# A chunked recurrence's triangular inverses: blocks of 16 in place of 32, a further merge, and the transfers on GpSimd's queue

## The chip, the cores and the metric

One core of one Trainium2 chip runs the whole layer in float32. The metric is the device time of one execution in microseconds. Three runs of the kernel before gave 1290.92, 1291.6 and 1295.13; the median is 1291.6.

## The reference

```python
def reference(x, ...):                        # x: (1, 1024, 1024), one layer
    h = rmsnorm(x, norm_mix_g); p = h @ w_in
    p_rwkv = p[..., :1792] + (token_shift(p_rwkv) - p_rwkv) * shift_mu
    y_rwkv = rwkv7_group(p_rwkv, ...)         # 8 heads of 64
    y_conv = conformer_conv_group(p[..., 1792:], ...)   # GLU, 31 taps, 512 channels, LayerNorm, SiLU
    x = x + concatenate([y_rwkv, y_conv]) @ w_out
    h = rmsnorm(x, norm_mlp_g)
    x = x + square(relu(h @ w_ff1)) @ w_ff2   # 1024 -> 4096 -> 1024
    return rmsnorm(x, norm_final_g)

def rwkv7_recurrence(r, decay, k, v, a, b):   # one step of 1024, per head
    sa = einsum('bhvk,bhk->bhv', S, a_t)
    S = S * w_t + sa ⊗ b_t + v_t ⊗ k_t
    y = einsum('bhvk,bhk->bhv', S, r_t)
```

The recurrence is what the change is about.

## The kernel before

The recurrence is done in chunks of 64 tokens, 16 chunks in a row. Inside a chunk the rank-one updates are collected in a unit triangular matrix of 64 by 64 for each head, whose inverse Th is needed before the chunk can be applied to the state. The eight heads are two groups, g = 0 and 1, of four heads (two head pairs p each); the tokens are two halves, h = 0 and 1, of eight chunks.

The stages, and what leaves each:

- `in_proj` multiplies the normalised input by a block of 128 columns of w_in, with three products of high and low halves (names hh, hl of the input, wh, wl of the weights), into a PSUM bank (ca, cb, ya, yb, ...). `mix_block` makes r, k and v of a pair from it, `conv_block(0..3)` the gated channels h2 of the convolution. Each projection's h goes into 48 long DVE operations per block, the taps (`do_taps`), which sum into `acc`.
- `decays` and `stage1(p, h)`, four pairs by two halves: from r, k, v the triangular products (AM, of KB and AR) and other factors. They go to DRAM: am_d (triangular blocks), lk_d, v_d, bon_d, n2_d (norms). These stores stand on `nc.sync`, SP's queue.
- `solve(g, (0, 1))`, once for each group when the pairs of that group are done: the tile Q holds 128 blocks of 32 by 32, one block on a partition (two halves by two diagonal blocks by 8 chunks by 4 heads). Thirty steps of two DVE operations each (L528 a product into Qt, L530 a sum) invert them; L524 and L532 scale by the norms. Q comes from am_d, nup from n2_d, the result goes to qd_d.
- `merge(g, h)`: reads two 32-blocks (QS) and the block off the diagonal (MX), transposes the first (QT), and joins them with 32 + 32 matmuls of 32 by 32 (MX·QT, copied to PT, then PT·QS) into a 64 by 64 inverse in th_d. Transfers of solve and merge alternate between `nc.sync` and `nc.scalar`.
- `step(g)`: one chunk of one group's chain: `fetch` (LK, rhs, and TA, which holds Th) on `nc.sync`, then matmuls L1·rhs, a copy to SR, Th·R (the rows SR,TA: the hop with th), a copy to rhs, KB·rhs, and a DVE addition that gives the next rhs; results y to y_d. A chain is 16 steps in a row.
- `conv_norm` transposes all four blocks' `acc` (rows ident,acc), then the output projection (w_out in 128-row pieces), the MLP, and the last norm follow.

What sets the order: a scheduler places all instructions at build time by priorities (`tc.high_priority`, where solve and merges of both groups have offset HP, chain steps HP and 2·HP) and by data; each engine then runs its list in that order, and each DMA queue its own. The calls are written so: conv_block(2), solve(0), merge(0, 0), merge(0, 1), steps of chain 0 between the projections of pairs 2 and 3, conv_block(3), solve(1), merge(1, 0), and steps and taps up to merge(1, 1) and conv_norm. Taps written behind a solve are tied behind it (`gate["solve"]`, set by the solve's last operation). The pool `mp` gives r, k, v, AM, kt, kd and the like their buffers: AM has two, kt (shared with vt) one.

Of the kernel before, what the change touches and what calls it, by code (L numbers as in the profile page):

```python
# [18 lines left out]
P = 128  # L19
# [16 lines left out]
EB = 1  # L36
# [16 lines left out]
def hymba_layer(ctx: ExitStack, tc: tile.TileContext, a: dict, out: bass.AP):  # L53
# [361 lines left out]
    factors = {}  # L415

# [23 lines left out]
    def stage1(p, h):  # L440
# [15 lines left out]
        nc.sync.dma_start(out=n2_d[p // 2, h, :, 2 * (p % 2):2 * (p % 2) + 2, :].rearrange("c r s -> r c s"), in_=n2.rearrange("r (c s) -> r c s", c=8))  # L456
# [7 lines left out]
        for i in range(2):  # L464
            hs = slice(64 * i, 64 * i + 64)
            AM = mp.tile([P, 8, P], F32, name="AM", bufs=2)
            for q in range(2):
                b1 = bank("s1")
                for c in range(4):
                    b1.mm(b1.t[:, c * P:(c + 1) * P], KB[hs, 4 * q + c].rearrange("p j t -> p (j t)"), AR[hs, 4 * q + c, :], True, True)  # L470
                V.tensor_tensor(AM[:, 4 * q:4 * q + 4, :], b1.t.rearrange("p (c t) -> p c t", c=4),
                                mask[:, None, :].to_broadcast([P, 4, P]), op=ALU.mult)
            nc.sync.dma_start(out=am_d[:, p // 2, cs, 2 * (p % 2) + i, :], in_=AM[0:64])
            nc.sync.dma_start(out=lk_d[64:128, p // 2, cs, 2 * (p % 2) + i, :], in_=AM[64:128])
        for i in range(2):
            nc.sync.dma_start(out=lk_d[0:64, p // 2, cs, 2 * (p % 2) + i, :], in_=AR[64 * i:64 * i + 64])
        for q in range(2):
            kd = mp.tile([P, 4, P], F32, name="kd", bufs=1)
# [7 lines left out]
            nc.sync.dma_start(out=lk_d[:, p // 2, 8 * h + 4 * q:8 * h + 4 * q + 4, 4 + p % 2, :], in_=kt)  # L486
# [5 lines left out]
        for e in range(2):  # L492
            nc.sync.dma_start(out=v_d[:, p // 2, cs][:, e::2, p % 2, :], in_=vt[64 * e:64 * e + 64])
# [5 lines left out]
        nc.sync.dma_start(out=bon_d[:, 4 * h:4 * h + 4, p, :], in_=v.rearrange("p (q t) -> p q t", q=4))  # L499
# [9 lines left out]
    def solve_blocks(g, hs):  # L509

        R = 64 * len(hs)
        Q = sv.tile([P, 32, 32], F32, name="Q", bufs=1)[0:R]
        nup = small.tile([P, 32], F32, name="nup", bufs=1)[0:R]
        for k, h in enumerate(hs):
            for bl in range(2):
                p0, sl = k * 64 + bl * 32, slice(bl * 32, bl * 32 + 32)
                (nc.sync, nc.scalar)[bl].dma_start(
                    out=Q[p0:p0 + 32], in_=am_d[sl, g, 8 * h:8 * h + 8, :, sl].rearrange("s c n t -> (c n) s t"))
                nc.scalar.dma_start(out=nup[p0:p0 + 32], in_=n2_d[g, h, :, :, sl].rearrange("c n s -> (c n) s"))
        tmp = sv.tile([P, 256], F32, name="Qt", bufs=1)[0:R]  # L520
# [3 lines left out]
        V.tensor_tensor(Q, Q, nup[:, None, :].to_broadcast([R, 32, 32]), op=ALU.mult)  # L524
        for s in range(1, 31):
            n = 31 - s
            o = tmp[:, 0:s * n].rearrange("p (s t) -> p s t", s=s)
            V.tensor_tensor(o, Q[:, 0:s, s:s + 1].to_broadcast([R, s, n]),  # L528
                            Q[:, s:s + 1, s + 1:32].to_broadcast([R, s, n]), op=ALU.mult)
# [207 lines left out]
    def step(g):  # L737
# [4 lines left out]
        with tc.high_priority(offset=(1 + g) * HP):  # L742
# [8 lines left out]
            if c % 2 == 1:  # L751
# [608 lines left out]
```

## Time and profile before

| what | value |
|---|---|
| median of three runs | 1291.6 us |
| the profiled execution | 1291.95 us, span 1290.2 us |
| mean granted TensorE clock | 0.961 |
| instructions | 20800 |
| DMA on SP's, ACT's (hardware) queues | 181192 and 13056 packets |
| DMA on GpSimd's (software) queue | 128 packets |
| HBM traffic | 110.23 MB read, 49.84 MB written |

PE is TensorE's matmuls, PEld its weight loads, DVE VectorE, ACT ScalarE, POOL GpSimd, SP the engine that only issues transfers. A row of a timeline has start, duration, engine, line, operation, out<-in and shape; in a window row stand the busy time of each engine and the count in that stretch, then the clock that the throttle granted, the share of DMA and GB/s. The chain that ended last gives start, duration and what it was. Most of the work on PE is in single rows L96, the helper for matmuls (L99 that for transposes), so the tile names tell them apart.

### The profile page before, as it was taken

The page shows a single profiled execution, that of the slowest core. Times are in us where ns is not written, and L with a number is a line of the kernel's source. Part 1 is how long each engine was busy: PE and PEld are TensorE (multiplying, and loading weights), DVE is VectorE, ACT ScalarE, POOL GpSimd, SP SyncE. Part 2 cuts the span into 40 slices and gives each one's busy share as a digit, 9 for nine tenths or more (in the row PEclk, how much of TensorE's full clock was granted, in tenths as well). Part 3 has the DMA queues.
Part 4 walks back from the last instruction along what each step waited for, and adds up shares of the span by engine and source line. Part 5 has one row for each costly group of instructions (what it writes and reads, how often), then busy time and mean ns, then how long its engine had stood idle before and what let it go on. Part 6 is the DMA issues. An engine that isn't in the chain of part 4 may idle for free.

```text
span 1290.2 us, 20800 instructions
## 1 busy us (share of the span) xinstructions
PE 1217.5 (94%) x8107; PEld 1052.2 (82%) x8107; DVE 944.8 (73%) x1639; ACT 558.0 (43%) x1001; POOL 107.4 (8%) x57
## 2 busy tenths in 40 slices
PE   5999999998999688999999899999997999999996
PEld 4999898887888577999988788888876788888885
DVE  6479696789549945664668766665459898897997
ACT  6432433333441166333468455455562333333344
POOL 1000000000000000000000000000015234242310
PEclk9999999997997586999999999999999999999999
DMA  5213426455464555734225454443276425232003
GB/s 191 58 50 98 125 62 176 113 139 123 118 168 130 129 143 165 216 111 123 78 88 184 152 164 153 150 146 109 87 268 217 142 66 164 65 101 79 17 1 131
DMA packets 194475, 161.44 MB, mean 125 GB/s; under 512 B 54386, under 2 KB 153784, under 8 KB 194376
## 3 DMA queue, kind: packets, MB, share of 16 engines
q1 hardware_dynamic: 181192, 157.90, 41.5%
q10 hardware_dynamic: 13056, 2.13, 0.9%
q8 instruction: 64, 1.05, 0.3%
q14 instruction: 35, 0.29, 0.1%
q0 software_dynamic: 128, 0.08, 0.0%
HBM read 110.23 MB, written 49.84 MB: 124 GB/s over the span
## 4 chain that ended last, share of the span: by engine, by line
PE 61%; DVE 9%; DMA 4%; ACT 2%; issue 1%; SPq 0%; ACTq 0%; DVEq 0%
PE ps L96 27%; PE yb L96 9%; PE ya L96 8%; PE cb L96 7%; PE ca L96 6%; PE pr L96 3%; DVE bl L852 2%; DVE al L852 2%; DVE sA L1190 1%; DVE x L1221 1%; PE ps L99 1%; DMA woraw<-in_w_out_dram 1%; DMA th_d<-QS 1%; DVE Q L530 1%; DVE Qt L528 1%
## 5 line engine op out<-in xcount | busy, mean ns | idle before, releaser
L851 ACT ACTIVATE ah<-sA 128x1024 fp32r<-128x1024 f32 x32 | 33.9, 1061 | 120.9 <-PE yb L96 48.0
L96 PE MATMUL cb<-hh,wh 128*128 128x256 f32 x248 | 72.8, 293 | 1.5 <-ACT hh L243 1.5
L96 PE MATMUL cb<-hl,wh 128*128 128x256 f32 x248 | 73.0, 294 | 0.3 <-DVE hl L244 0.3
L96 PE MATMUL cb<-hh,wl 128*128 128x256 f32 x248 | 71.8, 290 | 0.0
L96 PE MATMUL ps<-bh,ah 128*128 128x512 f32 x168 | 64.5, 395 | 5.6 <-ACT ah L851 3.5
L96 PE MATMUL ps<-bh,al 128*128 128x512 f32 x168 | 65.0, 391 | 3.2 <-DVE al L852 3.2
L96 PE MATMUL ps<-bl,ah 128*128 128x512 f32 x168 | 66.3, 395 | 1.5 <-DVE bl L852 1.5
L96 PE MATMUL yb<-hh,wh 128*128 128x256 f32 x232 | 67.7, 292 | 0.0
L96 PE MATMUL yb<-hh,wl 128*128 128x256 f32 x232 | 66.6, 287 | 0.0
L96 PE MATMUL yb<-hl,wh 128*128 128x256 f32 x232 | 66.5, 287 | 0.0
L851 ACT ACTIVATE w1h<-s 128x512 fp32r<-128x512 f32 x64 | 40.3, 632 | 52.6 <-PE ps L96 34.0
L852 DVE TENSOR_TENSOR al<-sA,ah 128x1024 fp32r<-128x1024 f32 x32 | 48.0, 1506 | 19.6 <-ACT ah L851 19.5
L852 DVE TENSOR_TENSOR w1l<-s,w1h 128x512 fp32r<-128x512 f32 x64 | 44.0, 688 | 24.8 <-ACT w1h L851 24.7
L1190 POOL TENSOR_TENSOR sB<-B,B11e 128x1024 f32<-128x1024 f32 x4 | 12.5, 3134 | 541.6 <-DVE al L852 539.3
L96 PEld LDWEIGHTS cb<-hh,wh 128*128 128x128 f32 x248 | 48.5, 195 | 5.4 <-ACT hh L243 1.9
L871 ACT ACTIVATE c<-c 128x512 f32<-128x512 f32 x60 | 37.9, 632 | 33.4 <-DVE c L957 20.1
L96 PEld LDWEIGHTS cb<-hl,wh 128*128 128x128 f32 x248 | 48.3, 195 | 4.8 <-issue 4.0
L96 PEld LDWEIGHTS cb<-hh,wl 128*128 128x128 f32 x248 | 48.2, 194 | 2.3 <-issue 2.1
L851 ACT ACTIVATE w1h<-w1r 128x512 fp32r<-128x512 f32 x48 | 30.2, 631 | 42.5 <-PE ps L96 26.6
L852 DVE TENSOR_TENSOR w1l<-w1r,w1h 128x512 fp32r<-128x512 f32 x48 | 32.9, 688 | 19.7 <-ACT w1h L851 19.7
L96 PEld LDWEIGHTS yb<-hh,wh 128*128 128x128 f32 x232 | 44.6, 192 | 3.1 <-issue 2.1
L96 PEld LDWEIGHTS yb<-hh,wl 128*128 128x128 f32 x232 | 44.6, 192 | 1.6 <-issue 1.5
(472 smaller groups left out, 4029.4 us busy)
## 6 DMA issues: line engine op xcount, KB each, us to landing
w1r<-in_w_ff_dram SPq DMA_DIRECT2D x44, 512.0 KB
hid_d<-c SPq DMA_DIRECT2D x64, 256.0 KB
LK<-lk_d SPq DMA_DIRECT2D x32, 384.0 KB
A<-hid_d SPq DMA_DIRECT2D x24, 512.0 KB
B<-in_w_ff_dram SPq DMA_DIRECT2D x24, 512.0 KB
wraw<-in_w_in_dram SPq DMA_DIRECT2D x22, 512.0 KB
xt<-in_x_dram SPq DMA_DIRECT2D x8, 512.0 KB
lk_d<-AR SPq DMA_DIRECT2D x16, 256.0 KB
```

Of the source, the lines that this page charges most:

```text
L96: return self._order(PE.matmul(o, lhsT=lhsT, rhs=rhs, start=start, stop=stop, skip_group_check=more))
L99: self._order(PE.transpose(o, in_, identity))
L528: V.tensor_tensor(o, Q[:, 0:s, s:s + 1].to_broadcast([R, s, n]), Q[:, s:s + 1, s + 1:32].to_broadcast([R, s, n]), op=ALU.mult)
L530: V.tensor_tensor(Q[:, 0:s, s + 1:32], Q[:, 0:s, s + 1:32], o, op=ALU.add)
L851: S.activation(hi, src, AF.Copy)
L852: V.tensor_tensor(lo, src, hi.bitcast(F32), op=ALU.subtract)
L871: S.activation(c, c if src is None else src, AF.Relu)
L1190: engine.tensor_tensor(t, x, y, op=op)
L1221: V.tensor_tensor(o, o, banks[t].t, op=ALU.add)
```

## The change

It does three things.

The solve takes blocks of 16. A partition's 32 by 32 block now holds two diagonal blocks of 16, and one DVE operation handles both (views Q16, four dimensions). There are 14 steps in place of 30. The upper half off the diagonal stays zero: Qf is cleared once by GpSimd and only the diagonal blocks are loaded, with eight transfers in place of four.

The merge has a first stage. AD holds three blocks from am_d (the two 32-blocks and the one off the diagonal, twelve loads in place of four). 64 matmuls 32 by 32 (AD·QT), a copy, 64 matmuls 32 by 16 (AD·QS) and a masked addition (`upper` keeps the rows of the first 16) make 32-blocks of the 16s; a second transpose and the 32 + 32 matmuls of before follow. So 192 matmuls for 64 in each of four merges.

All stores of stage 1, all transfers of solve and merges, and the stores of y to y_d are issued by `G.dma_start`, GpSimd's queue: twelve for each of eight stage-1 blocks, 16 for each solve, 17 for each merge, twelve of y. `fetch`, with the loads of Th into TA, stays on SP. kd shares a buffer with Ei.

The diff, cut to its core:

```diff
+    Qf = sv.tile([P, 1056], F32, name="Q")
+    G.memset(Qf, 0.0)
+    Q32 = Qf[:, 0:1024].rearrange("p (s t) -> p s t", t=32)
+    Q16 = Qf.rearrange("p (b r) -> p b r", b=2)[:, :, 0:512].rearrange("p b (s t) -> p b s t", t=32)[:, :, :, 0:16]
+    upper = const.tile([P, 1], F32, name="upper")
+    V.tensor_reduce(out=upper, in_=ident.rearrange("p (x e s) -> p x e s", e=2, s=16)[:, :, 0], op=ALU.add, axis=mybir.AxisListType.XY)
...
-            nc.sync.dma_start(out=am_d[:, p // 2, cs, 2 * (p % 2) + i, :], in_=AM[0:64])
-            nc.sync.dma_start(out=lk_d[64:128, p // 2, cs, 2 * (p % 2) + i, :], in_=AM[64:128])
+            G.dma_start(out=am_d[:, p // 2, cs, 2 * (p % 2) + i, :], in_=AM[0:64])
+            G.dma_start(out=lk_d[64:128, p // 2, cs, 2 * (p % 2) + i, :], in_=AM[64:128])
...
-            kd = mp.tile([P, 4, P], F32, name="kd", bufs=1)
+            kd = mp.tile([P, 4, P], F32, name="kd", tag="Ei", bufs=EB)
...
-        nc.sync.dma_start(out=bon_d[:, 4 * h:4 * h + 4, p, :], in_=v.rearrange("p (q t) -> p q t", q=4))
+        G.dma_start(out=bon_d[:, 4 * h:4 * h + 4, p, :], in_=v.rearrange("p (q t) -> p q t", q=4))
...
     def solve_blocks(g, hs):
-        Q = sv.tile([P, 32, 32], F32, name="Q", bufs=1)[0:R]
...
-                (nc.sync, nc.scalar)[bl].dma_start(
-                    out=Q[p0:p0 + 32], in_=am_d[sl, g, 8 * h:8 * h + 8, :, sl].rearrange("s c n t -> (c n) s t"))
...
+                p0, o = k * 64 + bl * 32, bl * 32
+                for e in range(2):
+                    sl, te = slice(o + 16 * e, o + 16 * e + 16), slice(16 * e, 16 * e + 16)
+                    G.dma_start(
+                        out=Q32[p0:p0 + 32, te, te], in_=am_d[sl, g, 8 * h:8 * h + 8, :, sl].rearrange("s c n t -> (c n) s t"))
+                G.dma_start(out=nup[p0:p0 + 32], in_=n2_d[g, h, :, :, o:o + 32].rearrange("c n s -> (c n) s"))
...
-        V.tensor_tensor(Q, Q, nup[:, None, :].to_broadcast([R, 32, 32]), op=ALU.mult)
-        for s in range(1, 31):
-            n = 31 - s
-            o = tmp[:, 0:s * n].rearrange("p (s t) -> p s t", s=s)
-            V.tensor_tensor(o, Q[:, 0:s, s:s + 1].to_broadcast([R, s, n]),
-                            Q[:, s:s + 1, s + 1:32].to_broadcast([R, s, n]), op=ALU.mult)
-            V.tensor_tensor(Q[:, 0:s, s + 1:32], Q[:, 0:s, s + 1:32], o, op=ALU.add)
-        V.memset(Q.rearrange("p s t -> p (s t)")[:, ::33], 1.0)
-        gate["solve"] = V.tensor_tensor(Q, Q, nup[:, :, None].to_broadcast([R, 32, 32]), op=ALU.mult)
+        nu = nup.rearrange("p (b s) -> p b s", b=2)
+        V.tensor_tensor(Q, Q, nu[:, :, None, :].to_broadcast([R, 2, 16, 16]), op=ALU.mult)
+        for s in range(1, 15):
+            n = 15 - s
+            o = tmp[:, 0:2 * s * n].rearrange("p (b s t) -> p b s t", b=2, s=s)
+            V.tensor_tensor(o, Q[:, :, 0:s, s:s + 1].to_broadcast([R, 2, s, n]),
+                            Q[:, :, s:s + 1, s + 1:16].to_broadcast([R, 2, s, n]), op=ALU.mult)
+            V.tensor_tensor(Q[:, :, 0:s, s + 1:16], Q[:, :, 0:s, s + 1:16], o, op=ALU.add)
+        V.memset(Qf[0:R, 0:1024:33], 1.0)
+        gate["solve"] = V.tensor_tensor(Q, Q, nu[:, :, :, None].to_broadcast([R, 2, 16, 16]), op=ALU.mult)
         for k, h in enumerate(hs):
             for bl in range(2):
                 p0 = k * 64 + bl * 32
-                (nc.sync, nc.scalar)[bl].dma_start(out=qd_d[g, h, bl], in_=Q[p0:p0 + 32])
+                G.dma_start(out=qd_d[g, h, bl], in_=Q32[p0:p0 + 32])
     def merge_blocks(g, h):
...
-        MX = sv.tile([P, 8, 32], F32, name="MX", bufs=1)
-        for x in range(4):
...
+        AD = sv.tile([P, 3, 8, 32], F32, name="AD", bufs=1)
+        for i, (r, c) in enumerate(((0, 0), (32, 32), (0, 32))):
+            for x in range(4):
+                G.dma_start(out=AD[32 * x:32 * x + 32, i], in_=am_d[r:r + 32, g, 8 * h:8 * h + 8, x, c:c + 32])
+        QS = sv.tile([P, 2, 8, 32], F32, name="QS", bufs=1)
         for bl in range(2):
-            (nc.sync, nc.scalar)[bl].dma_start(out=QS[:, bl], in_=qd_d[g, h, bl].rearrange("(j x) s t -> (x s) j t", x=4))
...
+        QT = sv.tile([P, 2, 8, 32], F32, name="QT", bufs=1)
+        V.transpose(QT.rearrange("p b j t -> p (b j t)"), QS.rearrange("p b j t -> p (b j t)"))
...
+        rows = [slice(32 * x, 32 * x + 32) for x in range(4)]
+        b2 = bank("s1")
+        for bl in range(2):
+            for j in range(8):
+                for r in rows:
+                    b.mm(b.t[r, bl * 256 + j * 32:bl * 256 + j * 32 + 32], AD[r, bl, j, :], QT[r, bl, j, :], True, True)
+        S.copy(AD[:, 0:2].rearrange("p b j t -> p (b j t)"), b.t)
+        for bl in range(2):
+            for j in range(8):
+                for r in rows:
+                    b2.mm(b2.t[r, bl * 128 + j * 16:bl * 128 + j * 16 + 16], AD[r, bl, j, :], QS[r, bl, j, 16:32], True, True)
+        up = QS[:, :, :, 16:32].rearrange("p b j t -> p (b j) t")
+        V.scalar_tensor_tensor(up, b2.t[:, 0:256].rearrange("p (n t) -> p n t", t=16), upper, up, op0=ALU.mult, op1=ALU.add)
+        V.transpose(QT[:, 0].rearrange("p j t -> p (j t)"), QS[:, 0].rearrange("p j t -> p (j t)"))
         for j in range(8):
-            for x in range(4):
...
+            for r in rows:
+                b.mm(b.t[r, j * 32:j * 32 + 32], AD[r, 2, j, :], QT[r, 0, j, :], True, True)
+        S.copy(AD[:, 0].rearrange("p j t -> p (j t)"), b.t[:, 0:256])
...
-            (nc.sync, nc.scalar)[i % 2].dma_start(out=th_d[g, h, bl, :, :, :, cb:cb + 32].rearrange("x s j t -> (x s) j t"), in_=QS[:, i])
+        for i, (src, bl, cb) in enumerate(((QS[:, 0], 0, 0), (QS[:, 1], 1, 32), (AD[:, 1], 0, 32))):
+            G.dma_start(out=th_d[g, h, bl, :, :, :, cb:cb + 32].rearrange("x s j t -> (x s) j t"), in_=src)
...
-                    nc.sync.dma_start(out=y_d[:, g, d], in_=y)
+                    G.dma_start(out=y_d[:, g, d], in_=y)
```

How the order moves, at three places. First PE's row where group 0 takes its first hop with th (SR,TA) among the projections (out yb, from the halves hh and hl of the input and wh, wl of the weights). Before:

```order
L96 MATMUL yb<-hh_165,wh 128x256
L96 MATMUL yb<-hl_166,wh 128x256
L96 MATMUL yb<-hh_165,wl 128x256
L96 MATMUL yb<-hh_169,wh 128x256
L96 MATMUL yb<-hl_170,wh 128x256
L96 MATMUL yb<-hh_169,wl 128x256
L96 MATMUL ca<-SR,TA 64x64 x4
L96 MATMUL ps<-AR,KB 128x128 x12
```

and after, where ya<-QT,AD are products of group 0's second merge:

```order
L96 MATMUL yb<-hh_165,wh 128x256
L96 MATMUL ca<-SR,TA 64x64 x2
L96 MATMUL ya<-QT,AD 32x32
L96 MATMUL ca<-SR,TA 64x64 x2
L96 MATMUL ya<-QT,AD 32x32
L96 MATMUL yb<-hl_166,wh 128x256
L96 MATMUL yb<-hh_165,wl 128x256
L96 MATMUL yb<-hh_169,wh 128x256
L96 MATMUL ya<-QT,AD 32x32
```

Behind the first merge's last products (out ca, from QS) stand 41 rows up to the hop before, and 20 after; the second merge, which stood behind the hop and a projection, now begins inside it. Up to the end of the last projection stand seven groups SR,TA before and nine after.

Second, DVE's row where the solve of group 1 (Qt, Q, nup) meets h of the last projection (L316). Before:

```order
L528 TENSOR_TENSOR Qt<-Q 128x228
L530 TENSOR_TENSOR Q<-Q,Qt 128x12x19
L316 SCALAR_TENSOR_TENSOR h_4194<-th,cb 128x256x2
L528 TENSOR_TENSOR Qt<-Q 128x234
L318 TENSOR_TENSOR h_4194<-h_4194 128x256
L330 TENSOR_SCALAR acc<-h_4194,cw,par_103 128x512
L530 TENSOR_TENSOR Q<-Q,Qt 128x13x18
```

and after:

```order
L316 SCALAR_TENSOR_TENSOR h_4447<-th,cb 128x256x2
L318 TENSOR_TENSOR h_4447<-h_4447 128x256
L330 TENSOR_SCALAR acc<-h_4447,cw,par_103 128x512
L645 TENSOR_TENSOR rhs<-ca,SR 64x256
L331 SCALAR_TENSOR_TENSOR acc<-h_4447,cw,acc 128x512
L629 TENSOR_TENSOR SR<-rhs,PC 64x256
L533 TENSOR_TENSOR Q<-Q,nup 128x2x16x16
L331 SCALAR_TENSOR_TENSOR acc<-h_4447,cw,acc 128x512
L537 TENSOR_TENSOR Qt<-Q 128x28
```

Before, twelve of the thirty steps stand ahead of h; after, the whole solve stands behind it, with taps and chain operations between its steps.

Third, PE's row ahead of the transposes of the last tapped block (ident,acc), where cb<-SR,TA are group 1's hops with th and pr or ps with QS the second merge of group 1. Before:

```order
L96 MATMUL cb<-SR,TA 64x64 x4
L96 MATMUL pr<-QS,PT 32x32 x24
L96 MATMUL cb<-rhs,LK 64x64 x4
L96 MATMUL yb<-rhs,TA 64x64 x4
L96 MATMUL pr<-QS,PT 32x32 x8
L96 MATMUL ca<-rhs,LK 64x64 x4
L96 MATMUL ya<-rhs,TA 64x64 x4
L99 MATMUL ps<-ident,acc 128x128 x3
```

and after:

```order
L96 MATMUL cb<-SR,TA 64x64 x4
L96 MATMUL ps<-QS,AD 32x16 x24
L96 MATMUL cb<-rhs,LK 64x64 x4
L96 MATMUL yb<-rhs,TA 64x64 x4
L96 MATMUL ps<-QS,AD 32x16 x14
L96 MATMUL cb<-rhs,LK 64x64 x4
L96 MATMUL yb<-rhs,LK 64x64 x4
L96 MATMUL ps<-QS,AD 32x16 x13
L96 MATMUL ca<-rhs,LK 64x64 x4
L96 MATMUL ya<-rhs,LK 64x64 x4
L99 MATMUL ps<-ident,acc 128x128 x12
```

Two hops of group 1 precede the transposes before, three after.

On GpSimd's own list for group 1, six stores of y and the last stage-1 stores stand ahead of the four stores of qd_d; then come two loads of QS, stores of th, and the twelve AD loads of the second merge.

More of the change, by code (lines that the diff above doesn't have):

```diff
@@ L455, in stage1 @@
         S.copy(n2, bn.t[0:2, :])
-        nc.sync.dma_start(out=n2_d[p // 2, h, :, 2 * (p % 2):2 * (p % 2) + 2, :].rearrange("c r s -> r c s"), in_=n2.rearrange("r (c s) -> r c s", c=8))
+        G.dma_start(out=n2_d[p // 2, h, :, 2 * (p % 2):2 * (p % 2) + 2, :].rearrange("c r s -> r c s"), in_=n2.rearrange("r (c s) -> r c s", c=8))
         kq = mp.tile([P, 512], F32, name="kq", bufs=1)
@@ L485, in stage1 @@
             S.copy(kt.rearrange("p c n -> p (c n)"), bk.t)
-            nc.sync.dma_start(out=lk_d[:, p // 2, 8 * h + 4 * q:8 * h + 4 * q + 4, 4 + p % 2, :], in_=kt)
+            G.dma_start(out=lk_d[:, p // 2, 8 * h + 4 * q:8 * h + 4 * q + 4, 4 + p % 2, :], in_=kt)
         bv = bank("s1")
@@ L492, in stage1 @@
         for e in range(2):
-            nc.sync.dma_start(out=v_d[:, p // 2, cs][:, e::2, p % 2, :], in_=vt[64 * e:64 * e + 64])
+            G.dma_start(out=v_d[:, p // 2, cs][:, e::2, p % 2, :], in_=vt[64 * e:64 * e + 64])
         S.activation(r, r, AF.Copy, scale=prm("r_k", p))
@@ L515, in solve_blocks @@
             for bl in range(2):
-                p0, sl = k * 64 + bl * 32, slice(bl * 32, bl * 32 + 32)
-                (nc.sync, nc.scalar)[bl].dma_start(
-                    out=Q[p0:p0 + 32], in_=am_d[sl, g, 8 * h:8 * h + 8, :, sl].rearrange("s c n t -> (c n) s t"))
-                nc.scalar.dma_start(out=nup[p0:p0 + 32], in_=n2_d[g, h, :, :, sl].rearrange("c n s -> (c n) s"))
-        tmp = sv.tile([P, 256], F32, name="Qt", bufs=1)[0:R]
+                p0, o = k * 64 + bl * 32, bl * 32
[4 more added lines that the diff above has]
+                G.dma_start(out=nup[p0:p0 + 32], in_=n2_d[g, h, :, :, o:o + 32].rearrange("c n s -> (c n) s"))
+        Q = Q16[0:R]
+        tmp = sv.tile([P, 112], F32, name="Qt", bufs=1)[0:R]
         V.tensor_scalar(nup, nup, 1e-24, None, op0=ALU.max)
@@ L548, in merge_blocks @@
-        PT = sv.tile([P, 8, 32], F32, name="PT", bufs=1)
+            G.dma_start(out=QS[:, bl], in_=qd_d[g, h, bl].rearrange("(j x) s t -> (x s) j t", x=4))
+        QT = sv.tile([P, 2, 8, 32], F32, name="QT", bufs=1)
+        V.transpose(QT.rearrange("p b j t -> p (b j t)"), QS.rearrange("p b j t -> p (b j t)"))
         b = bank((("ca", "ya"), ("cb", "pr"))[g][h])
+        rows = [slice(32 * x, 32 * x + 32) for x in range(4)]
[4 more added lines that the diff above has]
+                    b.mm(b.t[r, bl * 256 + j * 32:bl * 256 + j * 32 + 32], AD[r, bl, j, :], QT[r, bl, j, :], True, True)
@@ L559, in merge_blocks @@
-        S.copy(QS[:, 2].rearrange("p j t -> p (j t)"), b.t[:, 256:512])
-        for i, bl, cb in ((0, 0, 0), (1, 1, 32), (2, 0, 32)):
-            (nc.sync, nc.scalar)[i % 2].dma_start(out=th_d[g, h, bl, :, :, :, cb:cb + 32].rearrange("x s j t -> (x s) j t"), in_=QS[:, i])
+            for r in rows:
+                b.mm(b.t[r, 256 + j * 32:288 + j * 32], AD[r, 0, j, :], QS[r, 1, j, :], True, True)
+        S.copy(AD[:, 1].rearrange("p j t -> p (j t)"), b.t[:, 256:512])
+        for i, (src, bl, cb) in enumerate(((QS[:, 0], 0, 0), (QS[:, 1], 1, 32), (AD[:, 1], 0, 32))):
+            G.dma_start(out=th_d[g, h, bl, :, :, :, cb:cb + 32].rearrange("x s j t -> (x s) j t"), in_=src)
```

12 lines of the change are left out of this document (1 added, 11 removed).

## The prediction

> **What bounds the kernel now.** I read the page's engine rows and its 40 slices first, then stretches of 20 us around solve and merges, then the chain that ended last, then single rows of the work that the change touches.
>
> ```profile
> PE 1217.5 (94%) x8107; PEld 1052.2 (82%) x8107; DVE 944.8 (73%) x1639; ACT 558.0 (43%) x1001; POOL 107.4 (8%) x57
> PE   5999999998999688999999899999997999999996
> PEclk9999999997997586999999999999999999999999
> ```
>
> PE is busy 94% of the 1290.2 us span. A slice is 32 us; both rows drop in the thirteenth to the sixteenth, so the time that can be won or lost without more or less PE work lies at about 400 to 510 us. The stretches (columns: busy time and count of PE, PEld, DVE, ACT, POOL, then granted clock, DMA share, GB/s):
>
> ```profile
> 260.00:280.00 20.00, 20.00 (x164) 18.63 (x163) 17.72 (x42) 5.46 (x12) 0.11 (x1) 1.00 0.35 94
> ...
> 380.00:400.00 20.00, 19.93 (x189) 18.01 (x187) 11.89 (x33) 3.83 (x10) 0.00 (x0) 1.00 0.61 156
> 400.00:420.00 20.00, 17.22 (x163) 15.15 (x164) 18.95 (x47) 3.66 (x10) 0.00 (x0) 0.66 0.48 132
> 420.00:440.00 20.00, 13.21 (x240) 11.80 (x238) 18.48 (x38) 2.58 (x7) 0.30 (x1) 0.60 0.60 142
> 440.00:460.00 20.00, 15.04 (x227) 13.50 (x226) 15.05 (x27) 4.42 (x12) 0.00 (x0) 0.50 0.46 99
> 460.00:480.00 20.00, 16.69 (x201) 13.84 (x200) 9.59 (x31) 13.06 (x26) 0.00 (x0) 0.97 0.59 167
> 480.00:500.00 20.00, 13.78 (x104) 11.35 (x104) 11.32 (x32) 13.93 (x26) 0.00 (x0) 0.66 0.59 169
> 500.00:520.00 20.00, 18.84 (x157) 17.28 (x158) 12.71 (x24) 10.72 (x20) 0.00 (x0) 0.83 0.59 180
> 520.00:540.00 20.00, 20.00 (x193) 18.57 (x192) 13.63 (x39) 7.74 (x17) 0.00 (x0) 1.00 0.87 262
> ```
>
> Around group 0's solve (260 to 280) and up to 400 PE has no gap: work that leaves DVE there brings nothing, work added on PE costs all of itself. From 400 to 520 PE idles 120 − 94.8 = 25.2 us and has a clock of 0.50 to 0.97: here the end of group 1's chain of transfers and the taps decide when PE is full again, and from 520 on it is full. What stands in that stretch, in order of time, from the chain that ended last:
>
> ```profile
> 378.89 4.43 DMA am_d<-AM
> ...
> 388.05 1.24 DVE Q L524
> 397.92 1.04 DVE h L316
> ...
> 423.91 3.21 DMA qd_d<-Q
> 427.15 4.15 DMA QS<-qd_d
> ...
> 436.07 1.05 PE cb L96 x64
> ...
> 440.03 2.56 DMA th_d<-QS
> 442.61 1.95 DMA TA<-th_d
> 444.69 1.09 PE cb L96 x8
> ```
>
> The last projection ends, its h (397.92) opens the last block's taps, the solve ends at 423.91, two transfers, a merge, two transfers, and at 444.69 group 1 takes its first hop with th. From h to that hop: 46.8 us. The run profiled took 1291.95 us, span 1290.2; the median of the three runs is 1291.6, so I sum against 1291.95 and the difference of 0.35 is nothing.
>
> **Solve on DVE.** Sixty small operations (thirty steps) become 28 (fourteen), each of 2·s·(15−s) elements, thus 28 to 112, and its two multiplications go from 1024 to 512 elements.
>
> ```profile
> 225.00:290.00 65.00, 22.23 (x63) 1.00 0.52 126
> 380.00:430.00 50.00, 22.08 (x63) 0.80 0.58 154
> 389.76 0.22 DVE L528 TENSOR_TENSOR Qt<-Q 128x58 f32<-128x58 f32 x1
> 390.82 0.27 DVE L528 TENSOR_TENSOR Qt<-Q 128x108 f32<-128x108 f32 x1
> 425.31 0.41 DVE L624 TENSOR_TENSOR rhs<-ca,SR 64x256 f32<-64x256 f32 x1
> 438.24 0.73 DVE L331 SCALAR_TENSOR_TENSOR acc<-h,cws,acc 128x512 f32<-128x512 f32 x1
> ```
>
> The first two rows are tile Q alone on DVE in each group's stretch. Of 0.19 to 0.27 each, 28 take 6.7 us; two of 512 elements, by the tap's 0.73, 1.4; with the memset 8.2. So 22.1 becomes 8.2 per group, −13.9. For group 0 that is hidden under PE's 20.00 of 20: 0. For group 1 it depends on what stands between. Before, twelve of the thirty steps ran from 388.05 on, ahead of h. By the new order the solve begins behind h, with 11 taps and 10 chain operations among it up to its end: 8.2 + 11·0.73 + 10·0.41 + 2 (h and first taps) = 22.3, where it was 26.0 from h to the end.
>
> **Merges on PE.** Four products of 32 by 32 or 32 by 16 blocks, thrice the matmuls: 64 become 192, and 32 of them show as 64 passes.
>
> ```profile
> 292.42 0.75 PE L96 MATMUL ca<-QS,PT 32*32 32x32 f32 x64
> 293.10 0.38 PE L96 MATMUL yb<-hh,wh 128*128 128x256 f32 x1
> ```
>
> The next matmul starts 0.68 later: 10.6 ns a pass at full clock. 256 passes more are 2.7 us per merge; should 16 columns cost half, 2.0. Both merges of group 0 lie where PE has no gap: +5.4 (bounds 4.0 and 5.4; I take the row's). Group 1's run at the half clock (1.05 for 64 passes above): the first one's own way from transfers to th is two transposes, two sums or copies more, and four products, 10.2 us (2.1, 0.6, 2.1, 0.9, then twice 1.05 with a copy of 0.4, 0.9 the first transpose, the rest hand-overs), where before about 8.7 lay from 431.3 to 440.03.
>
> **Transfers on GpSimd's queue.** The page before has only four such:
>
> ```profile
> prow<-in_conv_w_dram POOLq DMA_DIRECT2D x1, 62.0 KB, 6.9
> prow<-in_norm_mix_g_dram POOLq DMA_DIRECT2D x1, 4.0 KB, 4.4
> ```
> ```profile
> 3.05 0.55 POOL L171 DMA_DIRECT2D prow<-in_conv_w_dram  x1
> ```
>
> Landing took 4.4 and 6.9 us, in the crowded start; an issue 0.55. On SP and ACT's queues the moved kinds take 2.56 to 4.43 in the chain above. The bounds for one hop are thus 0 and about +3; I take 0 for the flight, since 4.43 and 4.4 are near each other at like load, and the issues: qd_d's four and QS's four (the two that the first merge needs come first) now stand in one queue, where two shared them, +3 issues = +1.6. The Trainium skill's page "DMA: Bandwidth & Descriptors", section Latency and other measured facts, gives about 1 us to the first byte for GpSimd's software path and about 0.6 for the hardware one. By it, as an estimate, five hops would add 2 us; the rows allow that and more. The twelve stores of a stage-1 block leave SP's queue, and SP's fetches and weight loads get by sooner: 0, since PE has no gap there; they are issued by POOL, which is busy 8%, 12·0.55 = 6.6 us a block. ACT waits for kt's buffer behind them; ACT is busy 5.46 of 20, so 0 too, unless the landing grows to several times its length. y_d's stores stand ahead of qd_d's in POOL's order, and behind ACT's copies; 0, since those copies belong to earlier steps.
>
> **Where PE waits first.** Group 0's first hop with th:
>
> ```profile
> 294.37 4.39 DMA th_d<-QS
> ...
> 299.24 4.40 DMA TA<-th_d
> 303.77 0.65 PE ca L96 x8
> ```
> ```profile
> 300.00:320.00 20.00, 16.23 (x201) 14.69 (x202) 20.00 (x33) 6.05 (x17) 0.11 (x1) 0.66 0.64 136
> ```
>
> PE stood some 3.8 us, and the mean granted clock of these 20 us is 0.66: 0.34·20 = 6.8 us were lost by it. From the merge's last product (up to 293.1) to the hop are 10.6 us. The new order puts one chain group (0.65) and 19 passes of a projection between them, 0.12 each (x164 in the 20 us from 260): 3. So PE would wait 7.5, +3.5; the half clock behind it as before. Behind the hop, and mixed with it, stand products of the second merge. Its tile AD has one buffer, so its twelve loads go out when the first merge's th store has landed, at 0.55 each: the last that the first product needs lands 4.4 (issues) and 4.4 (landing) behind that, a few us after the hop. Bounds: the wait is gone (−3.5 − 3.8 − 6.8 = −14.1 from my value), or those loads hold PE 5 us longer.
>
> **The sum.** Two of group 0's chain steps move ahead of the last projection's end, nine hops with th instead of seven. A step is five groups of eight passes, as
>
> ```profile
> 342.90 0.61 PE ca L96 x8
> ```
>
> each: 3.0 a step, +6.0 before h. They are work taken from later, where PE idles, so I give no credit for it. h comes 5.4 + 6.0 + 3.5 = 14.9 later. From h to group 1's first hop with th: 22.3 + 7.4 (qd_d, QS as before) + 1.6 + 10.2 + 4.7 (th, TA as before) = 46.2 against 46.8. At the transposes of the last tapped block
>
> ```profile
> 458.37 0.90 PE L99 MATMUL ps<-ident,acc 128*128 128x128 f32 x3
> ```
>
> two steps of group 1 were done in 13.7 us; the new order has three ahead, thus 6.9 later, but the chain is then one step further: 0. Sum 14.9 − 0.6 = +14.3: 1291.95 + 14.3 = 1306.
>
> **Rivals.** First, no change: the first hop's wait goes, because GpSimd's queue, free of weight loads, gets the th stores out earlier. Then h moves by 14.9 − 14.1 = +0.8: 1292. For it: th's two transfers took 4.4 each there and 2.56 and 1.95 for group 1, so there is something to win. Against it: the hop stands nearer to the merge. Chance 0.18.
>
> Second, faster: not group 1's hops but the taps decide when PE is full again. DVE is at 18.95 and 18.48 of 20 from 400 to 440, and 13.9 us less there bring conv_norm forward. Together with a first wait that is gone: 0.8 − 13.9, about 1279. It decides from the point where h is less than 13 us late. Against it: at 460 to 480 DVE is down to 9.59 of 20 and PE still waits. Chance 0.19, mostly at 1279 to 1287.
>
> Third, slower still: GpSimd's transfers land late. With 6.9 for qd_d (3.21), QS (4.15) and th (2.56), 10.8 more on group 1's path, and 2.5 each for th and AD at the first hop: 1306 + 15.8 = 1322. For it: the only rows of that queue. Against it: they lie in the first 10 us. Chance 0.20. The Trainium skill's page "SBUF — State Buffer", section SBUF: two separate sides, says that GpSimd can't write descriptors while DVE runs an operation that takes both ports, and that a transfer of 620 ns then takes about 3100; its section Who interferes with whom says that tensor_tensor has no such mode. No run before shows GpSimd's transfers beside a busy DVE.
>
> **How the numbers follow.** My forecast has 0.43, 1298 to 1313 by its own bounds (merge passes 4.0 and the moved steps wholly hidden below, AD's loads +5 and +2 of flight above). A measurement here tells 0.3%, 3.9 us, from no change. Slower: 0.43 + 0.20 = 0.63; same 0.18; faster 0.19. The range leaves out a tenth at either end: up to the late landings, 1325, and down into the second rival, 1281.
>
> **What would show it.** Tile Q on DVE at some 8.2 us per group; h of the last projection at some 413; group 1's first hop with th at 459; PE waiting some 7 us at the first hop of group 0; PE idle in 400 to 520 not much less than 25 us. Wrong, if h comes before 404 or that first wait is under 2 us (then no change or faster), or if POOL's landings are above 6 us (then 1320 and more), or if stage 1's ACT work waits for kt and PE shows gaps before 380.

## The result: 49 us slower, and the profile after

The changed kernel takes 1340.39 us (median of 4 runs, 1338.59 to 1344.31) against 1291.26 for the kernel before (1290.92 to 1295.13): ratio 1.038, 95% interval 1.0361 to 1.0398. The forecast was 1306, with a range to 1325. The direction was right; 34 us were missing.

The engines and slices of the page after:

```profile
PE 1238.7 (92%) x9131; PEld 1073.6 (80%) x9131; DVE 926.0 (69%) x1584; ACT 560.4 (42%) x1005; POOL 240.8 (18%) x266
PE   5999999968999378899999899999997999999996
PEclk9999999976999557799999999999999899999998
```

DVE's busy time fell by 944.8 − 926.0 = 18.8 us, PE's rose by 21.2. But PE has two holes in place of one: the ninth slice (around 285 us) and the fourteenth to sixteenth (about 435 to 535 us), both with a lower clock. The same stretches as shown of before, and the two at the first hole (columns: busy time and count of PE, PEld, DVE, ACT, POOL, clock, DMA share, GB/s):

```profile
260.00:280.00 20.00, 18.05 (x445) 16.58 (x447) 19.99 (x32) 7.24 (x15) 1.80 (x2) 1.00 0.17 49
280.00:300.00 20.00, 11.24 (x192) 10.11 (x192) 16.82 (x28) 4.64 (x10) 10.98 (x17) 0.66 0.41 100
...
440.00:460.00 20.00, 8.14 (x278) 7.51 (x282) 18.32 (x37) 0.59 (x1) 4.14 (x6) 0.51 0.28 68
460.00:480.00 20.00, 5.99 (x187) 5.21 (x179) 11.83 (x19) 1.48 (x4) 8.65 (x13) 0.50 0.19 50
480.00:500.00 20.00, 17.48 (x313) 15.69 (x313) 3.25 (x8) 3.52 (x9) 3.82 (x7) 0.50 0.47 125
500.00:520.00 20.00, 18.24 (x318) 15.74 (x316) 8.04 (x26) 10.84 (x21) 2.59 (x3) 0.76 0.29 80
520.00:540.00 20.00, 14.78 (x123) 12.16 (x123) 11.70 (x34) 13.65 (x26) 1.10 (x2) 0.67 0.62 171
```

From 440 to 480 PE works 14.1 of 40 us, at half clock; before it was 31.7. The first hole, in PE's and DVE's timelines (start, duration, operation; in brackets the idle time before it and what ended it):

```profile
290.81 0.58 PE L96 MATMUL yb<-hh,wh 128*128 128x256 f32 x1 [7.27 <-DVE k L257]
```
```profile
288.09 0.76 DVE L331 SCALAR_TENSOR_TENSOR acc<-h,cw,acc 128x512 f32<-128x512 f32 x1
288.75 0.75 DVE L331 SCALAR_TENSOR_TENSOR acc<-h,cws,acc 128x512 f32<-128x512 f32 x1
289.42 0.71 DVE L557 STREAM_TRANSPOSE QT<-QS 128x512 f32<-128x512 f32 x1
290.04 0.72 DVE L257 SCALAR_TENSOR_TENSOR k<-yb,omu,pm 128x512 f32<-128x512 f32 x1
```

PE waits 7.27 us for bank yb, which the operation L257 frees (it makes k of a projection from yb). DVE works without a pause all that time: from 283.04 to 290.04 six taps (L331) and four other operations stand ahead of L257 in its list. Group 0's solve ends at 250.2 us, where it ended at 278.2 before; so the taps tied behind it come sooner, and stand where they hold up a projection. The second hole, group 1's first merge on PE, DVE and GpSimd's queue:

```profile
455.25 1.93 PE L96 MATMUL cb<-QT,AD 32*32 32x32 f32 x128 [9.93 <-DVE QT L557]
...
467.89 1.08 PE L96 MATMUL cb<-QT,AD 32*32 32x32 f32 x64 [7.41 <-DVE QT L572]
...
477.50 1.08 PE L96 MATMUL cb<-SR,TA 64*64 64x64 f32 x8 [5.30 <-DMA TA<-th_d]
```
```profile
423.73 1.04 DVE L316 SCALAR_TENSOR_TENSOR h<-th,cb 128x512 f32<-128x512 f32 x1 [5.15 <-PE cb L96]
...
444.42 0.69 DVE L541 TENSOR_TENSOR Q<-Q,nup 128x512 f32<-128x512 f32 x1
...
454.49 0.70 DVE L557 STREAM_TRANSPOSE QT<-QS 128x512 f32<-128x512 f32 x1
...
465.68 0.48 DVE L571 SCALAR_TENSOR_TENSOR QS<-ps,upper,QS 128x256 f32<-128x256 f32 x1
...
467.40 0.44 DVE L572 STREAM_TRANSPOSE QT<-QS 128x256 f32<-128x256 f32 x1
```
```profile
445.40 2.31 POOL L545 DMA_DIRECT2D qd_d<-Q  x4 [7.07 <-DVE Q L541]
448.17 1.83 POOL L555 DMA_DIRECT2D QS<-qd_d  x2 [0.46 <-issue]
...
470.93 1.78 POOL L555 DMA_DIRECT2D QS<-qd_d  x2 [2.74 <-PE cb L96]
472.70 0.89 POOL L582 DMA_DIRECT2D th_d<-AD  x1
```

The merge's three DVE operations stand among taps of 0.66 us each, so PE waits 7.41 us for a masked sum (L571) and a transpose (L572) that take 0.92 together. From the first transpose (454.49) to the store of th (472.70) go 18.2 us. And the transposes of the tapped blocks:

```profile
504.83 1.40 PE L99 MATMUL ps<-ident,acc 128*128 128x128 f32 x9
```

458.37 before, 504.83 after: +46.5, nearly all of the 49.9 between the spans (1290.2, 1340.1). GpSimd's transfers (KB each, median us from issue to landing):

```profile
lk_d<-AM POOLq DMA_DIRECT2D x16, 256.0 KB, 4.4
qd_d<-Q POOLq DMA_DIRECT2D x8, 128.0 KB, 2.6
QS<-qd_d POOLq DMA_DIRECT2D x8, 128.0 KB, 2.9
th_d<-QS POOLq DMA_DIRECT2D x8, 128.0 KB, 2.7
th_d<-AD POOLq DMA_DIRECT2D x4, 128.0 KB, 5.0
```

All but the last land as the hardware queues' did in the chain before (2.56 to 4.43). The last, th_d<-AD, is the third store of each merge: 5.0 is the median of four, and in group 1's first merge it took 2.8.

The marks, in us of the profiled executions, for the kernels told of below (h: start of the last projection's h on DVE; hop: group 1's first hop with th; last transposes: the first row of conv_norm's that holds some of the last tapped block):

| kernel | us | ratio to before, 95% | h | hop | last transposes |
|---|---|---|---|---|---|
| before | 1291.3 | 1 | 397.9 | 444.7 | 458.4 |
| changed | 1340.4 | 1.0361 to 1.0398 | 423.7 | 477.5 | 504.8 |
| e1, hardware queues | 1322.0 | 1.0230 to 1.0285 | 416.0 | 463.1 | 487.9 |
| e2, queue change alone | 1288.1 | 0.9965 to 0.9997 | 386.7 | 443.8 | 453.2 |
| e8, short solve alone | 1280.5 | 0.9885 to 0.9938 | 404.1 | 435.7 | 445.5 |
| e9, long merge alone | 1345.8 | 1.0392 to 1.0458 | 426.6 | 487.7 | 512.7 |
| e5a, one tie | 1322.2 | 1.0228 to 1.0273 | 414.0 | 467.9 | 493.5 |
| e5b, both ties | 1322.9 | 1.0227 to 1.0280 | 414.3 | 461.4 | 488.3 |
| e18, second merge late | 1318.5 | 1.0197 to 1.0272 | 421.2 | 475.0 | 468.7 |
| e13, see below | 1300.5 | 1.0063 to 1.0115 | 412.4 | 450.3 | 457.3 |

From the last transposes to the end of the span go 827 to 835 us in all of these but e18 (846) and e13 (840), where the second merge of group 1 is moved behind them. So in these kernels the lateness at that mark is nearly the whole lateness.

### The profile page after: what moved, and what is told of

It reads as the page before. It is cut to its first block, busy times and chain, and to the rows that moved or that the text cites. A ratio compares the mean times of both kernels' runs of the same rounds, so it can differ in the third digit from the quotient of the medians.

```text
span 1340.1 us, 22893 instructions
## 1 busy us (share of the span) xinstructions
PE 1238.7 (92%) x9131; PEld 1073.6 (80%) x9131; DVE 926.0 (69%) x1584; ACT 560.4 (42%) x1005; POOL 240.8 (18%) x266
## 4 chain that ended last, share of the span: by engine, by line
PE 81%; DVE 10%; DMA 3%; ACT 3%; issue 2%; POOL 0%; SPq 0%; DVEq 0%; ACTq 0%; POOLq 0%
PE ps L96 29%; PE yb L96 14%; PE cb L96 12%; PE ya L96 11%; PE ca L96 8%; PE pr L96 3%; DVE acc L331 2%; PE ps L99 2%; DMA woraw<-in_w_out_dram 2%; DVE bl L873 1%; DVE al L873 1%; DVE odd L331 1%; DVE x L1242 1%; DVE sA L1211 1%; DMA lk_d<-kt 1%
## 5 line engine op out<-in xcount | busy, mean ns | idle before, releaser
L873 DVE TENSOR_TENSOR al<-sA,ah 128x1024 fp32r<-128x1024 f32 x32 | 51.3, 1605 | 19.5 <-ACT ah L872 19.5
L96 PEld LDWEIGHTS yb<-hh,wh 128*128 128x128 f32 x232 | 46.2, 199 | 11.0 <-DVE k L257 7.5
L96 PEld LDWEIGHTS yb<-hl,wh 128*128 128x128 f32 x232 | 46.1, 199 | 1.4 <-issue 1.1
```

Of the source, the lines that this page charges most:

```text
L96: return self._order(PE.matmul(o, lhsT=lhsT, rhs=rhs, start=start, stop=stop, skip_group_check=more))
L873: V.tensor_tensor(lo, src, hi.bitcast(F32), op=ALU.subtract)
```

## The experiments

**Which part costs: blocks and merge, or the queue.** Theory A: DVE's list, in which taps stand ahead of what PE waits for. Theory B: GpSimd's queue. e1 puts every transfer of the changed kernel back:

```diff
-            G.dma_start(out=am_d[...], in_=AM[0:64])          # and all stage-1 and y stores
+            nc.sync.dma_start(out=am_d[...], in_=AM[0:64])
-                G.dma_start(out=qd_d[g, h, bl], in_=Q32[p0:p0 + 32])   # and Q, QS, th_d; nup on scalar, AD on sync
+                (nc.sync, nc.scalar)[bl].dma_start(out=qd_d[g, h, bl], in_=Q32[p0:p0 + 32])
```

> The changed kernel with every transfer back on SP's and ACT's queues (stage stores and y on SP; solve and merges split as before); blocks of 16 and the longer merge stay. Theory A (DVE's list: taps stand ahead of the merge's two further DVE operations and of the operation that frees a projection's bank, and PE waits): DVE's list here is almost the same, so 1325 to 1345. Theory B (GpSimd's queue, with stores behind one another, makes the time): 1290 to 1305.

Measured 1322.0, ratio 1.0258. Below A's span and far from B's: 31.7 us of the loss need no GpSimd queue, some 18 come with it. The waits of the second hole are there with hardware queues too (PE's row at 454.29 waits 7.07 us for DVE's L572).

e2 is the other half, the queue without blocks of 16: in the kernel before, the same transfers to `G.dma_start`.

> The kernel before (blocks of 32, short merge) with stage stores, y stores and all transfers of solve and merges on GpSimd's queue. Theory A: 1290 to 1300. Theory B: 1315 to 1340.

Measured 1288.1, ratio 0.9981 (0.9965 to 0.9997): 2 us faster. B falls as a cause by itself: the same queue costs 18 us behind a long merge and nothing behind the short one. Two kernels split it by kind: e3 is the changed kernel with stage and y stores on `nc.sync`, e4 with solve's and merges' transfers on `nc.sync` and `nc.scalar` as in e1.

> The changed kernel with stage-1 and y stores back on SP's queue; solve's and merges' transfers stay on GpSimd's. 1340 with all on GpSimd's, 1322 with none. If the stage stores in one line (kt behind other transfers) make the 18 us: 1322. If solve's and merges' transfers on GpSimd make them: 1340. If it is DVE's order alone, that shifts with any change of queue: neither is bound to follow, and the wait of PE for k of about 7 us tells which.

> The other half: stage-1 and y stores on GpSimd's queue, solve's and merges' transfers on SP's and ACT's. Stage stores as the cause: 1340. Transfers of solve and merges as the cause: 1322. DVE's order alone: 1318 to 1340, by whether PE waits 7 us for k.

e3: 1332.9 (1.0298 to 1.0350), between its first two spans; e4: 1315.9 (1.0166 to 1.0226), below all of its own. With the merges on hardware queues, stage stores on GpSimd's gain 6; with the merges on GpSimd's they lose 8. Such a change of sign is not a price for a queue. The wait for k is shorter in e3, and gone in e4, where PE's longest wait for such an operation in 250 to 300 is 1.90 (for v). e3's row:

```profile
293.25 0.58 PE L96 MATMUL yb<-hh,wh 128*128 128x256 f32 x1 [4.59 <-DVE k L257]
```

So in the three kernels that use GpSimd's queue the wait and the time go together: 7.27 us and 1340, 4.59 and 1333, none and 1316. It is not all of it, since e1 has no such wait either and takes 1322. Which order results hangs on the queues, as the lists are built with them. The stage stores alone in the kernel before, e2s, gave

> The kernel before with stage-1 and y stores alone on GpSimd's queue. With all of them there it took 1288 against 1290; with the blocks of 16 the stage stores gained 6 with the merges on SP and ACT and lost 7 with them on GpSimd. If GpSimd's queue is worth something for stores: 1284 to 1288. If it only moves the order about: 1287 to 1297.

1293.8, ratio 1.0042 (1.0025 to 1.0058), 5 us slower: again no fixed sign.

**The first hole: taps ahead of a bank's release.** A tie makes the taps that are written behind an operation start only when that operation is done. e5a ties them behind the second transpose of the first merge in group 0, in place of the solve; e5b does so in both groups:

```diff
-        V.transpose(QT[:, 0]..., QS[:, 0]...)
+        tq = V.transpose(QT[:, 0]..., QS[:, 0]...)
+        if g == 0 and h == 0:          # e5b: if h == 0:
+            gate["solve"] = tq
```

> The changed kernel with one line: taps written behind the first merge of group 0 are tied behind its second transpose instead of behind the solve. Theory A: the 7.3 us wait of PE for the bank that DVE's k frees goes, and some of the half clock behind it; 1326 to 1334. Theory B: 1340, within 4.

> The same for the first merge of both groups. Theory A: group 1's merge takes 10 to 12 us from the landing of QS to the store of th instead of 20, so another 8 to 10 less than with group 0 alone; 1316 to 1326, unless the last block's taps, which now start later, end last: then 1326 to 1334. Theory B: 1340, within 4.

e5a: 1322.2, 18 us less than the changed kernel and more than was expected, with GpSimd's queue untouched. PE's wait for k falls to 0.98; the hop with th waits instead:

```profile
285.61 1.09 PE L96 MATMUL ca<-SR,TA 64*64 64x64 f32 x8 [5.92 <-DMA TA<-th_d]
```

so h comes 9.7 us earlier; the other 8 came later on. e5b: 1322.9, no more. Its mechanism worked, as its rows show:

```profile
450.85 1.08 PE L96 MATMUL cb<-QT,AD 32*32 32x32 f32 x64 [1.06 <-DVE QT L572]
...
461.42 1.09 PE L96 MATMUL cb<-SR,TA 64*64 64x64 f32 x8 [6.26 <-DMA TA<-th_d]
```

The wait for L572 is 1.06 in place of 7.76 (in e5a), the hop 6.4 us earlier, the last transposes 5.2: and the end the same. I supposed that the taps, which start later, end last; e10b leaves 12 of the last block's 48 taps out of e5b.

> The kernel with taps tied behind both first merges (1322.9), with 12 of the last block's 48 taps left out, 8 us of DVE. There group 1's first hop came 6 us earlier than with one tie and the time did not change. If the taps, which start later there, now end last: 1314 to 1318. If not: 1321 to 1324.

Measured 1323.4 (1.0236 to 1.0290): no change. That supposition fell. In 520 to 600 PE idles 7.3 us in e5b and 2.6 in e5a, so the gain is given back there: PE waits 3.65 us for DVE's yo (L676, which makes the recurrence's output ready for the output projection) where e5a waits 0.79, and 2.67 for ACT's SR of the chain where e5a does not. Why those come later in e5b is not shown.

**Solve and merge apart.** e8 cuts the solve of the kernel before to its first 14 steps on half the width (the inverse is left unfinished), e9 has the long merge behind the old solve:

```diff
-        for s in range(1, 31):
-            n = 31 - s
+        for s in range(1, 15):            # e8; products and sums to column 16 in place of 32
+            n = 15 - s
```

> The kernel before with the solve cut to 14 of its 30 steps, on half the width (the inverse is left unfinished); merge and queues as before. It costs DVE about what the blocks of 16 cost, with no further merge. If the solve's DVE time lay on group 1's path (the prediction's second rival): 1274 to 1280. If it is mostly hidden, or given back by the order: 1284 to 1292.

> The 30-step solve of 32 by 32 blocks as before, with the longer merge (192 matmuls, four further DVE and ACT operations, twelve loads), on SP's and ACT's queues; the first stage of the merge is then applied to what is done already, so the values are not the inverse. If the longer merge is what costs (its DVE operations behind the taps, its passes on PE, the second merge in the chain): 1320 to 1336, as much as the blocks of 16 with these queues (1322) or up to 14 more. If the cost came from the solve's new place in DVE's order: 1300 or less.

e8: 1280.5, 10.3 us faster, just above the first span. So in the kernel before a good part of the solve's DVE time was on the path. e9: 1345.8, 55 us slower, above what was expected. Together (e1) they make +31.7, not −10 + 55: the order is another one each time.

```profile
476.38 0.48 DVE L569 SCALAR_TENSOR_TENSOR QS<-ps,upper,QS 128x256 f32<-128x256 f32 x1
478.10 0.44 DVE L570 STREAM_TRANSPOSE QT<-QS 128x256 f32<-128x256 f32 x1
```

In e9 as in the changed kernel, the sum and the second transpose come 11 to 13 us behind the first (465.19). By itself the merge is the part that costs.

**What stands ahead of the last block's transposes.** e11 is e4 with the tie of e5a; e13 adds this:

```diff
     do_taps(23)
     step(0)
-    merge(1, 1)
     ...
     cTs[0] = conv_norm(sc, ct, 0)
+    merge(1, 1)
 # in merge:
-        with tc.high_priority(offset=SOLVE_HP[g] * HP):
+        with tc.high_priority(offset=(SOLVE_HP[g] if (g, h) != (1, 1) else 0) * HP):
```

> Stage-1 and y stores on GpSimd's queue, solve's and merges' transfers on SP's and ACT's (1316 so far), and taps tied behind the first merge of group 0. If taps ahead of the operations that free banks cost only where PE waits for them: that kernel shows waits of 1 to 2 us, so 1311 to 1317. If the tie itself is worth 18 us whatever the queues: 1298.

> The same with the second merge of group 1 written behind the first conv_norm and without its priority, so the transposes of the last tapped block come ahead of group 1's second step in PE's list, not behind its third. If the steps and products ahead of those transposes are the cost (the prediction called a step ahead worth its 6.9 us): 1300 to 1308. If the step ahead is worth what it takes: 1311 to 1318, as without the move.

e11: 1311.2 (1.0138 to 1.0193); e13: 1300.5 (1.0063 to 1.0115), 11 us less, as the first of its spans said. e18 makes the move alone, in the changed kernel:

> The changed kernel with the second merge of group 1 alone written behind the first conv_norm, without its priority; all else as changed (1340). If the steps and products of group 1 ahead of the last block's transposes cost 11 or more here too: 1318 to 1330. If the wait ahead of group 1's first hop (PE 14 of 40 us busy in 440 to 480) decides alone: 1336 to 1342.

1318.5, 22 us less than the changed kernel. Its rows:

```profile
458.07 1.54 PE L99 MATMUL ps<-ident,acc 128*128 128x128 f32 x6
...
468.71 0.90 PE L99 MATMUL ps<-ident,acc 128*128 128x128 f32 x3 [0.64 <-DVE acc L336]
...
474.97 1.08 PE L96 MATMUL cb<-SR,TA 64*64 64x64 f32 x8 [3.27 <-DMA TA<-th_d]
```

The transposes now fill PE's wait for group 1's hop; the hop itself is only 2.5 us earlier. The last of them (468.71) start as soon as the last sum of the taps (L336) is done. In the kernel before and in the changed kernel that sum stands at

```profile
452.27 0.68 DVE L336 TENSOR_TENSOR acc<-acc,odd 128x512 f32<-128x512 f32 x1
470.50 0.68 DVE L336 TENSOR_TENSOR acc<-acc,odd 128x512 f32<-128x512 f32 x1
```

and the transposes at 458.37 and 504.83: they are ready 5.4 and 33.6 us before their turn in PE's list. That wait is what the move takes away. It does not all reach the end, since e18 takes 11 us longer from there on. The tie of e5a is worth 18 us and this move 22; their intervals overlap, so which of the two causes is the larger is not shown. In the kernel before the move brings nothing (e14, 1291.6, 0.9999 to 1.0034): nine of the transposes stood early there, and only two steps ahead of the rest.

> The kernel before with the same move. There only two steps and the short merge stand ahead of the transposes, so less is to be had: 1282 to 1289 if the transposes' time decides, 1289 to 1293 if not.

e16 ties the taps behind group 1's first merge too, in e13:

> The kernel at 1300 (stage stores on GpSimd's queue, tie behind group 0's merge, second merge late) with the tie for group 1's first merge too: its products stop waiting for DVE's taps, some 6 us, but the last block's taps start later. If group 1's first hop still decides there: 1293 to 1297. If taps and transposes decide: 1299 to 1306.

1296.1 (1.0025 to 1.0061): 4 us less than e13 by the medians; the two ran beside different runs of the kernel before, and their intervals do not overlap, if only just. Its hop is 4.1 us earlier (446.27), but its last transposes are 7.0 later (464.3), and its profiled execution (1299.45) is as long as e13's (1299.01); so it is not shown that the earlier hop is what gains the 4. Taken together, the queues of e4, both ties and the late second merge leave 6 of the 49 us.

**The price of a pass.** e17 does each matmul of the first stage twice in e13, e19 only in group 0's merges, e20 only in group 1's second:

```diff
-                for r in rows:
+                for r in rows + rows:     # e19: rows * (2 if g == 0 else 1); e20: (g, h) == (1, 1)
                     b.mm(...)
```

> The kernel at 1300 with each matmul of the merges' first stage done twice, 256 passes more per merge. If a pass costs 10.6 ns of full PE time wherever it stands, 4 times 2.7: 1308 to 1314. If they fall into PE's waits: 1299 to 1304.

> The kernel at 1300 with the first stage's matmuls doubled in the two merges of group 0 alone. If they cost their rows' time: 1304 to 1308. If the order of the work around them, and half clock behind new waits, cost as much again: 1310 to 1325.

> The same doubled in the second merge of group 1 alone. By their rows at half clock: 1303 to 1307. If they hold up each step of group 1's chain among which they stand: 1315 to 1335.

Against e13's median, e17: 1359.2 (1.0508 to 1.0551), +59, far above both of its spans. e19: 1313.0 (1.0140 to 1.0212), +12.5, with h 13.9 later. e20: 1344.7 (1.0387 to 1.0435), +44, also above both. Each ran beside other runs of the kernel before than e13 did, whose medians differ by 2 to 4 us; set against those, e19 is only 9 above e13. By their rows 256 passes take 2.7 us at full clock, 5.4 for group 0. So in group 0 they cost some 1.6 to 2.3 times their rows. In e20 the second merge, which has no priority, is late for the chain itself: group 1's ninth hop waits for its th (the eighth and ninth hop):

```profile
541.91 0.68 PE L96 MATMUL cb<-SR,TA 64*64 64x64 f32 x8
...
569.61 1.11 PE L96 MATMUL cb<-SR,TA 64*64 64x64 f32 x8 [3.04 <-DMA TA<-th_d]
```

Between the two lie 27.7 us, where the steps ahead of them took 8 to 16. e17 and e20 thus price a late merge more than a pass, and say nothing clean on the latter; why the ninth hop comes so much later than the passes explain was not traced further.

## Why the prediction was wrong, step by step

Three steps failed: where PE waits first (+3.5 us; PE's idle time up to h grew by 11.9), the merge's own way (10.2 us; it took 18.2), and the third chain step ahead of the transposes, put at 0 (it cost 13.6). What it said of the solve's length, of the added work on PE and of the landings held.

- **Solve on DVE, 8.2 us; h to its end 22.3.** Right: tile Q takes 8.22 and 8.02, and from 423.73 to 445.11 is 21.4. That it gains nothing in group 0 and 3.7 in group 1 is doubtful: in the kernel before, e8 puts a solve of this length at −10, near the second rival's −13.9. With the longer merge it was not measured by itself.
- **Group 0's first hop waits 7.5 (term +3.5).** Wrong place. At the hop PE does not wait (it starts at 294.53, right behind other work). PE waits 7.27 us ahead of the projection before the hop, for DVE's k behind taps. I had looked for what the new DVE order did only around group 1's solve. In e5a, where the wait for k is nearly gone, the hop waits 5.92 for th: what I forecast was there, hidden behind the other wait. With the waits that follow, PE's idle time from 20 us on to the last h is 17.2 against 5.3 before: +11.9, and the clock is 0.66 over 40 us in place of 20. (The 3.5 is also a slip: 7.5 less the 3.8 that I read is 3.7.)
- **Merge passes +5.4 and two chain steps +6.0 up to h.** About right as work: PE's busy time from 20 us on to h rose by 13.9, and the two make 11.4. What a pass costs beyond its row is open: doubling them costs 9 to 12.5 (e19), some of it in idle time.
- **h 14.9 later.** It is 25.8. Of the 10.9 that are missing, 2.5 are more work on PE and 8.4 more idle time (11.9 for 3.5).
- **The merge's own way, 10.2 us.** Wrong: 18.2 from the first transpose to th's store. I summed the operations' durations and called the rest hand-overs; but two of them are queued on a DVE that the taps fill. e5b, with nothing ahead of them, has 6.5 between first and second transpose; the changed kernel 12.9. In the sum this is the 7.6 us by which h to hop takes 53.8 in place of 46.2 (8.0 in the merge, −0.4 in the rest). It lies on the chain that ended last; but e5b takes most of it away and the end does not move, so it is not worth 7.6 by itself.
- **Third step ahead, "the chain is then one step further: 0".** Wrong, and the largest miss: it is no credit. PE's list puts three steps and most of the second merge ahead of conv_norm's transposes; hop to transposes takes 27.3 us where I had 20.6 and gave 6.9 of it back. The rest of the layer hangs on conv_norm then, not on the chain, and its transposes had been ready for 33.6 us: moving the second merge out of the way gives 22 us back (e18).
- **GpSimd's transfers at no cost of flight, an issue 0.55.** About right: landings 2.6 to 5.0, issues 0.58 (four in 2.31) to 0.92 (two in 1.83). The third rival's late landings did not happen. One cost of the order in that queue was left out: the last store of th (472.70) stands behind the two QS loads of the second merge (470.93), which had waited 2.74 us for PE, and these 1.77 us lie on the chain that ended last. The Trainium skill's page "SBUF — State Buffer", section Who interferes with whom, has tensor_tensor without a two-port mode. The trace does not test that rule cleanly, since DVE's work beside these transfers was mostly scalar_tensor_tensor (the taps): in 440 to 480 us, with DVE at 18.32 of 20 in the first half, qd_d's and QS's transfers landed in medians of 2.6 and 2.8.
- **ACT waits for kt: 0.** Not quite. Its store is issued 1.4 us behind the copy, after two others in GpSimd's list; ACT waits for it 5.36 us, and PE then 3.38 us for ACT's kt at 323.18:

```profile
322.55 0.59 ACT L491 COPY kt<-ps 128x512 f32<-128x512 f32 x1 [5.36 <-DMA lk_d<-kt]
```

Of the prediction's signs one misled. "That first wait is under 2 us (then no change or faster)" came true, for the hop did not wait, and the kernel is 49 us slower: the sign took for granted that a hop that does not wait comes early. The others: h came at 423.7 (some 413 was named), the hop at 477.5 (459), and PE idles 33.8 us in 400 to 520 (not much less than 25).

So in a sum: forecast +14.3; +10.9 because h is later than I had it; +7.6 for the merge on DVE; +13.6 to the last transposes (27.3 in place of 13.7); together 46.4 at the transposes, and 49.9 at the end.

What is open: the terms are taken from marks of single executions, and each experiment moved the whole order, so their effects do not add. That kd shares a buffer with Ei was never varied by itself; in the changed kernel's trace from 200 to 420 us no operation on Ei waits. Of the versions tried the kernel before with the queue change alone (e2) is the fastest that leaves nothing out, by 2 us; nothing with the longer merge beat the kernel before.

## What to carry to other kernels

An operation that is short in its row can cost its place in the queue: for each that a change adds, see what stands ahead of it on its engine and how full that engine is there, not only the sum of durations. Where work is reordered, compare the same point of the whole program in both orders, and give no credit for a step done earlier unless what ends last depends on it. If a change frees an engine, look at what moves into the free time and whom that now holds up.

## What the runs showed of the hardware

After some long bursts of small matmuls PE pauses, and the trace shows nothing that it waits for. In e17, PE's timeline (passes of 32 by 32 blocks, then the wait that the trace calls issue):

```profile
254.81 1.57 PE L96 MATMUL ca<-QT,AD 32*32 32x32 f32 x163 [0.47 <-DVE QT L557]
258.61 1.50 PE L96 MATMUL ca<-QT,AD 32*32 32x32 f32 x93 [2.22 <-issue]
263.66 1.36 PE L96 MATMUL ps<-QS,AD 32*32 32x16 f32 x141
265.96 1.15 PE L96 MATMUL ps<-QS,AD 32*32 32x16 f32 x115 [0.95 <-issue]
```

PE does 163 and 141 passes in 1.6 and 1.4 us, and then pauses for 2.22 and 0.95 us. Of the bursts of 64 passes in the kernel before none shows one; e1 has 2.8 us of such waits on tile ps and e9 1.5. Not every long burst is followed by one: the changed kernel does 128 passes at 265.03 in one row. What PE waits for there is not shown.

A 32 by 16 product took the time of a 32 by 32 one: in the changed kernel 128 passes took 1.26 us (269.43) and 1.29 us (265.03), at full clock.
